# Last quarter of a feed-forward in seven block products: shared sums taken into the residual ahead of the sixth product, and the final gain multiplied onto each half row before the row's scale

## The chip, the cores and the metric

The kernel runs on one core of a Trainium2 chip. The metric is the device time of one execution in microseconds (us); the median of three runs of the kernel before is 855.49 us.

## The reference

One layer of a streaming encoder on 512 rows of 1024 channels, all in float32: three attention branches are gated and merged, projected and added to the residual `h`; then comes a feed-forward sub-layer, and at the end a normalisation of every row. Only the last two matter here:

```python
u2 = rmsnorm(h, g_ffn[l])
h = h + jnp.square(jax.nn.relu(u2 @ w_ff1[l])) @ w_ff2[l]      # D_FF = 4096
...
return rmsnorm(h, g_final)        # h * rsqrt(mean(h*h) + EPS) * g_final
```

## The kernel before

**Precision.** A float32 product is made of three matmuls: each operand is split into a rounded part "hi" and a rest "lo" (`split`: ScalarE casts, VectorE subtracts, lines 202 and 203), and `mm3` (lines 150 to 152) adds hi·hi, hi·lo and lo·hi in one accumulator. Before TensorE can work on a weight tile of 128x1024 numbers, the tile must be loaded, cast by ScalarE (`hi`) and subtracted by VectorE (`lo`). There are three buffers for `hi` and three for `lo`.

**The feed-forward.** The 4096 inner channels are taken in four quarters, `q` = 0 to 3. Within a quarter both multiplications are done on 2x2 blocks with seven block products in place of eight (Strassen's scheme in Winograd's form), so that block sums of operands and results take the place of one product. For the second multiplication the result is the residual itself: `C(i, j, t)` is the half row (512 channels) number `j` of row tile `2*i + t` of `h`; the four tiles of 128 rows are `hN[0]` to `hN[3]`, written h0 to h3 below. `second_product` goes through the products in the order `SECOND` = 1, 2, 5, 3, 6, 7, 4. Each is 24 matmuls of 128x512 numbers: two weight tiles (`i` = 0, 1) of 12 matmuls each, which serve the row tiles `t` = 0 and then `t` = 1. The very last product (n = 4 of the last quarter) is run the other way about: all 12 matmuls of `t` = 0, then all 12 of `t` = 1, so both weight tiles are wanted within its first 7 matmuls.

**Where results go.** `evac` takes a finished product out of its accumulator. Products 1 and 5 stay in PSUM over all four quarters (`held`); products 6 and 7 are summed in the tiles `R6[t]` and `R7[t]` until the third quarter, and R7 is added to the residual ahead of the last quarter. In the last quarter, with M1 to M7 for the products (M1 and M5 over all quarters), R6 becomes M1 - R6 at product 1; at product 6 the tiles E = R6 - M6 and G = M5 - E are made, and G is added to `C(0, 1)` and `C(1, 1)`, E to `C(1, 0)`; at product 7, M7 is taken from `C(1, 1)` and added to `C(1, 0)`.

**The end of a row.** `finish(t, c, n)` is called once for each half row when its last sum is in (n = 0 for the first half that is done, n = 1 for the second). It squares the half on ScalarE, with the sum of the squares going to `hss` (`sumsq`, line 824). The first half is multiplied by `g_final` (`gl`) on VectorE. At the second half the mean goes to `ms` (VectorE, line 831) and its power -1/2 to `rr` (GpSimd, line 832); then VectorE multiplies the second half by `rr` and `gl` in one instruction (line 1057), ScalarE multiplies the first half by `rr` (line 1059), and each sends its half to `out`, by the queue of SyncE and by ScalarE's own.

**What sets the order.** TensorE's order is that of the code. On the other engines a scheduler orders the instructions when the program is built; on the chip each engine runs its queue in that order and waits, at an instruction whose input is not there, with all that is behind it. Two other things hang on VectorE's splits in this stretch: the weights of products 5, 6, 7 and 4 are sums of blocks, which GpSimd's queue makes by DMAs that add into the tiles `b11` and `b12` (line 1114) as soon as VectorE's subtraction has read the sum before.

Of the kernel before, what the change touches and what calls it, by code (L numbers as in the profile page):

```python
# [14 lines left out]
ALU = mybir.AluOpType  # L15
AX = mybir.AxisListType

P = 128
D = 1024
# [42 lines left out]
def hybrid_block(ctx, tc, chunks, wst, xT, memT, xN, cols, gffn, gfin, wup, cst, out):  # L62
    nc = tc.nc
# [758 lines left out]
    def sumsq(sq, src, t, c, n):  # L822

        nc.scalar.activation(sq, src[:, 512 * c:512 * c + 512], AF.Square, accum_out=hss[:, t, n:n + 1])
        if n == 0:
            nc.vector.tensor_scalar(hss[:, t, 0:1], hss[:, t, 0:1], 1.0 / D, EPS, op0=ALU.mult, op1=ALU.add)

    def rms_tile(pool_, t):
        ms = pool_.tile([P, 1], F32, tag="ms", name=nm("ms"), bufs=2)
        r = pool_.tile([P, 1], F32, tag="rr", name=nm("rr"), bufs=2)  # L830
        nc.vector.tensor_scalar(ms, hss[:, t, 1:2], 1.0 / D, hss[:, t, 0:1], op0=ALU.mult, op1=ALU.add)
        nc.gpsimd.tensor_tensor(r, ms, mhalf[:, :1], op=ALU.pow)
        return r

# [2 lines left out]
    with pool("outp") as op_:  # L837
# [50 lines left out]
        def half(j, i, ks=range(KT)):  # L888
            sl = slice(256 * i, 256 * i + 256)
            for k in ks:  # L890
                mm3(first[j][:, sl], ws[j][0][:, k, :], ws[j][1][:, k, :], *(x[:, 2 * (k // 4) + i, k % 4, :] for x in u2),
                    k == 0, k == KT - 1)
# [9 lines left out]
        half(1, 0, range(4, KT))  # L902
        half(0, 1)
        half(1, 1)

# [7 lines left out]
    with pool("ff") as yp:  # L915
# [9 lines left out]
        def scratch():  # L925
            return yp.tile([P, S], F32, tag="sq", name=nm("sq"), bufs=2)
# [118 lines left out]
                first_evac(n, i, ps)  # L1045


        def finish(t, c, n):

            sumsq(scratch(), hN[t], t, c, n)  # L1050
            h = [hN[t][:, 512 * g:512 * g + 512] for g in range(2)]
            g_ = [gl[:, 512 * g:512 * g + 512] for g in range(2)]
            if n == 0:
                nc.vector.tensor_tensor(h[c], h[c], g_[c], op=ALU.mult)
            else:
                r = rms_tile(yp, t)
                nc.vector.scalar_tensor_tensor(h[c], h[c], r, g_[c], op0=ALU.mult, op1=ALU.mult)
                nc.sync.dma_start(out[t * P:(t + 1) * P, 512 * c:512 * c + 512], h[c])
                nc.scalar.mul(h[1 - c], h[1 - c], r)
                nc.scalar.dma_start(out[t * P:(t + 1) * P, 512 - 512 * c:1024 - 512 * c], h[1 - c])  # L1060

        def C(i, j, t):
            return hN[2 * i + t][:, 512 * j:512 * j + 512]
# [1 line left out]
        def evac(q, n, t, ps):  # L1065
            last = q == NQ - 1
            if n == 1 and last:
                x = scratch()
                nc.scalar.copy(x, ps)
                add(C(0, 0, t), x)  # L1070
                sub(R6[t], x, R6[t])
            if n == 2:
                add(C(0, 0, t), ps)
                if last:
                    finish(t, 0, 0)
            if n == 3:
                add(C(0, 1, t), ps)
            if n in (6, 7) and not last:
                R = (R6 if n == 6 else R7)[t]
                if q == 0:  # L1080
                    nc.scalar.copy(R, ps)
                else:
                    add(R, ps)
            if n == 6 and last:
                E, G = R6[t], s1[t]
                sub(E, E, ps)
                sub(G, held[5][t], E)
                add(C(0, 1, t), G)
                finish(t, 1, 1)
                add(C(1, 1, t), G)  # L1090
                add(C(1, 0, t), E)
            if n == 7 and last:
                add(C(1, 1, t), ps, ALU.subtract)
                finish(2 + t, 1, 0)
                add(C(1, 0, t), ps)
            if n == 4:
                add(C(1, 0, t), ps)
                if last:
                    finish(2 + t, 0, 1)

# [154 lines left out]
```

## Time and profile before

| | |
|---|---|
| three runs | 855.39, 855.49, 856.64 us |
| profiled execution | 854.4 us, of which the span from the first to the last instruction is 852.6 us |
| busy in the span | TensorE 831.8 us (98%), VectorE 554.9 us (65%), ScalarE 438.9 us (51%), GpSimd 97.3 us (11%) |
| the chain that ended last | TensorE 86%, VectorE 6%, ScalarE 3%, DMA 3% of the span |

The profiled execution lies 1.1 us under the median of the runs; differences are taken against its own time and then carried to the median. A start in the timeline is counted from the first instruction; products 2, 5, 3, 6, 7, 4 of the last quarter run from about 808.5 us to 843 us. On VectorE an instruction of 128x512 numbers lasts 0.68 us in the profile but the next one starts 0.60 us after it, since two neighbours overlap a little; where instructions are queued, the distance of the starts is what one costs.

### The profile page before, as it was taken

The numbers are of one execution on the slowest core, as the hardware profiler recorded it, in microseconds if no ns is written. First come the engines' busy times: TensorE is split into PE (matmuls) and PEld (weight loads), VectorE is DVE, ScalarE is ACT, GpSimd is POOL, SyncE is SP. The second block draws the span as 40 slices with busy tenths as digits, with TensorE's granted clock in tenths as the row PEclk, the third lists the DMA queues.
The fourth block names the chain that finished last, engine by engine and source line by source line (L and its number), as shares of the span: only waits on it lengthen the run. The fifth ranks groups of instructions, "written<-read, shape, count | busy, mean of one in ns | idle before, by whom it ended". The sixth has DMA issues, their size and how long they took to land.

```text
span 852.6 us, 11738 instructions
## 1 busy us (share of the span) xinstructions
PE 831.8 (98%) x4473; PEld 708.0 (83%) x4473; DVE 554.9 (65%) x886; ACT 438.9 (51%) x703; POOL 97.3 (11%) x114
## 2 busy tenths in 40 slices
PE   7899999999999999999999999999999999999994
PEld 5768788888888888787888889888998899889983
DVE  5784667856344546475444446857689668877897
ACT  8764656755333333132333335655577467646754
POOL 5100000000000022222121100001001100110011
PEclk9999999999999999999999999999999999999998
DMA  8435665553646547156322421948756875895553
GB/s 319 154 124 191 181 211 160 153 194 118 178 127 182 185 125 223 50 173 181 141 102 95 148 100 39 280 111 200 238 192 157 214 244 166 188 246 196 149 90 108
DMA packets 35993, 141.40 MB, mean 166 GB/s; under 512 B 4448, under 2 KB 5408, under 8 KB 34208
## 3 DMA queue, kind: packets, MB, share of 16 engines
q1 hardware_dynamic: 27424, 93.44, 30.7%
q0 software_dynamic: 6720, 41.95, 23.0%
q10 hardware_dynamic: 1792, 5.26, 1.7%
q8 instruction: 35, 0.57, 0.3%
q14 instruction: 22, 0.18, 0.1%
HBM read 138.50 MB, written 27.30 MB: 194 GB/s over the span
## 4 chain that ended last, share of the span: by engine, by line
PE 86%; DVE 6%; ACT 3%; DMA 3%; issue 2%; SPq 0%; POOL 0%; POOLq 0%; ACTq 0%; DVEq 0%
PE mm L150 23%; PE mm L151 23%; PE mm L152 23%; PE a L151 3%; PE a L150 3%; PE a L152 3%; DMA nFb<-dF 1%; DVE h L932 1%; PE a L767 1%; DVE lo L203 1%; DMA raw<-in_wst_dram 1%; PE a L784 1%; DMA memr<-in_memT_dram 1%; PE a L527 1%; PE a L526 1%
## 5 line engine op out<-in xcount | busy, mean ns | idle before, releaser
L142 DVE TENSOR_TENSOR wlo<-raw,whi 128x1024 fp32r<-128x1024 f32 x79 | 100.5, 1276 | 99.0 <-ACT whi L141 98.3
L141 ACT CAST whi<-raw 128x1024 fp32r<-128x1024 f32 x79 | 83.0, 1053 | 127.9 <-PE mm L151 102.6
L150 PE MATMUL mm<-uhi,whi 128*128 128x512 f32 x352 | 139.8, 397 | 0.0
L152 PE MATMUL mm<-uhi,wlo 128*128 128x512 f32 x352 | 137.7, 391 | 0.2 <-DVE wlo L142 0.2
L151 PE MATMUL mm<-ulo,whi 128*128 128x512 f32 x352 | 137.6, 391 | 0.0
L202 ACT CAST hi<-raw 128x1024 fp32r<-128x1024 f32 x58 | 60.8, 1049 | 44.5 <-PE mm L151 31.7
L203 DVE TENSOR_TENSOR lo<-raw,hi 128x1024 fp32r<-128x1024 f32 x58 | 70.9, 1222 | 17.6 <-ACT hi L202 17.6
L152 PEld LDWEIGHTS mm<-uhi,wlo 128*128 128x128 f32 x352 | 66.2, 188 | 14.8 <-DVE wlo L142 0.6
L150 PEld LDWEIGHTS mm<-uhi,whi 128*128 128x128 f32 x352 | 66.3, 188 | 13.6 <-issue 0.7
L151 PEld LDWEIGHTS mm<-ulo,whi 128*128 128x128 f32 x352 | 66.3, 188 | 12.9
L203 DVE TENSOR_TENSOR lo<-b,hi 128x1024 fp32r<-128x1024 f32 x40 | 48.8, 1222 | 26.0 <-ACT hi L202 26.0
L202 ACT CAST hi<-b 128x1024 fp32r<-128x1024 f32 x40 | 41.9, 1048 | 44.5 <-PE mm L152 30.4
L151 PE MATMUL mm<-lo,ch 128*128 128x512 f32 x160 | 62.5, 391 | 0.9 <-DVE lo L203 0.9
L152 PE MATMUL mm<-hi,cl 128*128 128x512 f32 x160 | 62.3, 389 | 0.0
L150 PE MATMUL mm<-hi,ch 128*128 128x512 f32 x160 | 62.3, 389 | 0.0
L1114 POOL DMA_DIRECT2D b<-in_wst_dram x32 | 27.6, 864 | 273.8 <-DVE lo L203 230.0
L152 PE MATMUL mm<-u2h,lo 128*128 128x256 f32 x192 | 54.3, 283 | 0.0
L151 PE MATMUL mm<-u2l,hi 128*128 128x256 f32 x192 | 54.3, 283 | 0.0
L150 PE MATMUL mm<-u2h,hi 128*128 128x256 f32 x192 | 54.3, 283 | 0.0
L150 PE MATMUL mm<-u2sh,hi 128*128 128x256 f32 x144 | 40.8, 283 | 0.0
L151 PE MATMUL mm<-u2sl,hi 128*128 128x256 f32 x144 | 40.8, 283 | 0.0
L152 PE MATMUL mm<-u2sh,lo 128*128 128x256 f32 x144 | 40.8, 283 | 0.0
(349 smaller groups left out, 1936.5 us busy)
## 6 DMA issues: line engine op xcount, KB each, us to landing
raw<-in_wst_dram SPq DMA_DIRECT2D x122, 512.0 KB
b<-in_wst_dram POOLq DMA_DIRECT2D x32, 512.0 KB, 5.3
T<-in_wst_dram POOLq DMA_DIRECT2D x12, 1024.0 KB, 8.4
raw<-T SPq DMA_DIRECT2D x24, 512.0 KB
b<-in_wst_dram SPq DMA_DIRECT2D x16, 512.0 KB
nFb<-dF ACTq DMA_DIRECT2D x8, 512.0 KB
xr<-in_xT_dram SPq DMA_DIRECT2D x4, 512.0 KB
h<-in_xN_dram SPq DMA_DIRECT2D x4, 512.0 KB
```

Source lines behind the costliest of these rows:

```text
L141: cast = nc.scalar.copy(hi, raw)
L142: nc.vector.tensor_tensor(lo, raw, f(hi), op=ALU.subtract)
L150: nc.tensor.matmul(ps, lh, rh, start=start, stop=False)
L151: nc.tensor.matmul(ps, lh, rl, start=False, stop=False)
L152: nc.tensor.matmul(ps, ll, rh, start=False, stop=stop)
L202: nc.scalar.copy(hi, src)
L203: return nc.vector.tensor_tensor(lo, src, f(hi), op=ALU.subtract).ins
L526: nc.tensor.matmul(po[:, q0:], vv, PTh[:, c0:c0 + w], start=n == 0, stop=False)
L527: nc.tensor.matmul(po[:, q0:], vv, PTl[:, c0:c0 + w], start=False, stop=n == 3)
L767: nc.tensor.matmul(ps[:, t, :], kk[:, sl], qq[:, sl], start=True, stop=True)
L784: nc.tensor.matmul(po[r, t, :], qpos[e][:, 64 * c:64 * c + 64], prev[:, c, :], start=False, stop=True)
L1114: nc.gpsimd.dma_start(to[i], wst[index["B", q, i, x]], accum_op=ALU.add)
```

## The change

Four things are changed, all in the last quarter, and no matmul is among them.

1. M1 is copied into `R7[t]`, which is free by then; R6 is left as it is and M1 - R6 goes to `R7[t]`, and is added to `C(1, 0)` at once. When product 5 is done, M5 - R7 is made and added to `C(0, 1)` and `C(1, 1)`. Both stand ahead of product 6.
2. At product 6 only M6 itself is left: ScalarE copies it to `R6[t]` and it is added to `C(0, 1)`. At product 7, M7 - M6 is made, taken from `C(1, 1)` and added to `C(1, 0)`.
3. `finish` multiplies each half by `gl` into another tile (`od` for h0 and h1, `ev` for h2 and h3) while ScalarE squares the half; at the second half VectorE multiplies that tile by `rr` alone, and ScalarE does the same to the first half's tile. `scalar_tensor_tensor` goes out.
4. The addition of the last product to `C(1, 0)` of h3 is placed behind the mean (`ms`) of h2.

```diff
--- before.py
+++ after.py
@@ -825,10 +825,12 @@
         if n == 0:
             nc.vector.tensor_scalar(hss[:, t, 0:1], hss[:, t, 0:1], 1.0 / D, EPS, op0=ALU.mult, op1=ALU.add)
 
+    ms_end = [None]
+
     def rms_tile(pool_, t):
         ms = pool_.tile([P, 1], F32, tag="ms", name=nm("ms"), bufs=2)
         r = pool_.tile([P, 1], F32, tag="rr", name=nm("rr"), bufs=2)
-        nc.vector.tensor_scalar(ms, hss[:, t, 1:2], 1.0 / D, hss[:, t, 0:1], op0=ALU.mult, op1=ALU.add)
+        ms_end[0] = nc.vector.tensor_scalar(ms, hss[:, t, 1:2], 1.0 / D, hss[:, t, 0:1], op0=ALU.mult, op1=ALU.add).ins
         nc.gpsimd.tensor_tensor(r, ms, mhalf[:, :1], op=ALU.pow)
         return r
 
@@ -1045,19 +1048,21 @@
                 first_evac(n, i, ps)
 
 
+        hgs = {}
+
         def finish(t, c, n):
 
             sumsq(scratch(), hN[t], t, c, n)
-            h = [hN[t][:, 512 * g:512 * g + 512] for g in range(2)]
-            g_ = [gl[:, 512 * g:512 * g + 512] for g in range(2)]
-            if n == 0:
-                nc.vector.tensor_tensor(h[c], h[c], g_[c], op=ALU.mult)
-            else:
+            sl = slice(512 * c, 512 * c + 512)
+            hg = hgs[t, c] = (ev if t > 1 else od)[t % 2][:, n, :]
+            nc.vector.tensor_tensor(hg, hN[t][:, sl], gl[:, sl], op=ALU.mult)
+            if n:
                 r = rms_tile(yp, t)
-                nc.vector.scalar_tensor_tensor(h[c], h[c], r, g_[c], op0=ALU.mult, op1=ALU.mult)
-                nc.sync.dma_start(out[t * P:(t + 1) * P, 512 * c:512 * c + 512], h[c])
-                nc.scalar.mul(h[1 - c], h[1 - c], r)
-                nc.scalar.dma_start(out[t * P:(t + 1) * P, 512 - 512 * c:1024 - 512 * c], h[1 - c])
+                nc.vector.tensor_scalar(hg, hg, r, None, op0=ALU.mult)
+                nc.sync.dma_start(out[t * P:(t + 1) * P, sl], hg)
+                other = hgs[t, 1 - c]
+                nc.scalar.mul(other, other, r)
+                nc.scalar.dma_start(out[t * P:(t + 1) * P, 512 - 512 * c:1024 - 512 * c], other)
 
         def C(i, j, t):
             return hN[2 * i + t][:, 512 * j:512 * j + 512]
@@ -1065,10 +1070,16 @@
         def evac(q, n, t, ps):
             last = q == NQ - 1
             if n == 1 and last:
-                x = scratch()
+                x = R7[t]
                 nc.scalar.copy(x, ps)
                 add(C(0, 0, t), x)
-                sub(R6[t], x, R6[t])
+                sub(x, x, R6[t])
+                add(C(1, 0, t), x)
+            if n == 5 and last:
+                x = R7[t]
+                sub(x, ps, x)
+                add(C(0, 1, t), x)
+                add(C(1, 1, t), x)
             if n == 2:
                 add(C(0, 0, t), ps)
                 if last:
@@ -1082,19 +1093,21 @@
                 else:
                     add(R, ps)
             if n == 6 and last:
-                E, G = R6[t], s1[t]
-                sub(E, E, ps)
-                sub(G, held[5][t], E)
-                add(C(0, 1, t), G)
+                nc.scalar.copy(R6[t], ps)
+                add(C(0, 1, t), ps)
                 finish(t, 1, 1)
-                add(C(1, 1, t), G)
-                add(C(1, 0, t), E)
             if n == 7 and last:
-                add(C(1, 1, t), ps, ALU.subtract)
+                x = R6[t]
+                sub(x, ps, x)
+                add(C(1, 1, t), x, ALU.subtract)
+                add(C(1, 0, t), x)
                 finish(2 + t, 1, 0)
-                add(C(1, 0, t), ps)
             if n == 4:
-                add(C(1, 0, t), ps)
+                if last and t:
+                    with tc.issue_after(ms_end[0]):
+                        add(C(1, 0, t), ps)
+                else:
+                    add(C(1, 0, t), ps)
                 if last:
                     finish(2 + t, 0, 1)
```

The order of TensorE's matmuls is the same in both programs, and the queues of VectorE, ScalarE, GpSimd and SyncE are the same up to product 1 of the last quarter. The rows below are instructions in the order of an engine's queue: line, operation, output and inputs. A name's digits ahead of the last underscore are the program's (h0 is `hN[0]`, R70 `R7[0]`, b110 `b11[0]`, `od1` the second tile of `od`, `lo` and `hi` the parts of a weight tile); the number behind it is a buffer's.

VectorE around product 5 (weight tiles from `b110` and `b111`), up to the first weight tile of product 3 (from `raw`). Before:

```order
L932 TENSOR_TENSOR h1_3639<-h1_3639,sq_1057_7187 128x512
L929 TENSOR_TENSOR R61_4583<-sq_1057_7187,R61_4583 128x512
L929 TENSOR_TENSOR s11_4577<-ev1_4573,s11_4577 128x512
L203 TENSOR_TENSOR lo_1069_7253<-b110_4086,hi_1068_7252 128x1024
L203 TENSOR_TENSOR cl0_4580<-ev0_4572,ch0_4578 128x512
L932 TENSOR_TENSOR h0_3638<-h0_3638,mm_1058_7197 128x512
L929 TENSOR_TENSOR od1_4575<-od1_4575,s11_4577 128x512
L203 TENSOR_TENSOR lo_1071_7270<-b111_4087,hi_1070_7269 128x1024
L203 TENSOR_TENSOR cl1_4581<-s11_4577,ch1_4579 128x512
L932 TENSOR_TENSOR h1_3639<-h1_3639,mm_1059_7198 128x512
L203 TENSOR_TENSOR cl1_4581<-ev1_4573,ch1_4579 128x512
L203 TENSOR_TENSOR lo_1076_7294<-raw_1074_7291,hi_1075_7293 128x1024
```

and with the change:

```order
L932 TENSOR_TENSOR R70_4584<-R70_4584,R60_4582 128x512
L932 TENSOR_TENSOR R71_4585<-R71_4585,R61_4583 128x512
L932 TENSOR_TENSOR od1_4575<-od1_4575,s11_4577 128x512
L203 TENSOR_TENSOR cl0_4580<-ev0_4572,ch0_4578 128x512
L935 TENSOR_TENSOR h0_3638<-h0_3638,mm_1056_7197 128x512
L203 TENSOR_TENSOR lo_1069_7270<-b111_4087,hi_1068_7269 128x1024
L203 TENSOR_TENSOR cl1_4581<-s11_4577,ch1_4579 128x512
L935 TENSOR_TENSOR h2_3640<-h2_3640,R70_4584 128x512
L935 TENSOR_TENSOR h3_3641<-h3_3641,R71_4585 128x512
L935 TENSOR_TENSOR h1_3639<-h1_3639,mm_1057_7198 128x512
L203 TENSOR_TENSOR cl1_4581<-ev1_4573,ch1_4579 128x512
L203 TENSOR_TENSOR lo_1074_7300<-raw_1072_7297,hi_1073_7299 128x1024
```

The subtractions that make M1 - R6 have moved from ahead of `b110`'s tile to behind it, and the additions of M1 - R6 to h2 and h3 are new ahead of product 3's first tile.

VectorE at the two weight tiles of the last product (`b110` and `b111` as inputs). Before:

```order
L203 TENSOR_TENSOR lo_1103_7447<-b110_4086,hi_1102_7446 128x1024
L932 TENSOR_TENSOR h0_3638<-h0_3638,s10_4576 128x512
L932 TENSOR_TENSOR h2_3640<-h2_3640,s10_4576 128x512
L932 TENSOR_TENSOR h1_3639<-h1_3639,s11_4577 128x512
L932 TENSOR_TENSOR h3_3641<-h3_3641,s11_4577 128x512
L203 TENSOR_TENSOR lo_1105_7452<-b111_4087,hi_1104_7451 128x1024
L932 TENSOR_TENSOR h2_3640<-h2_3640,mm_1092_7395 128x512
```

and with the change:

```order
L935 TENSOR_TENSOR h0_3638<-h0_3638,mm_1078_7335 128x512
L935 TENSOR_TENSOR h1_3639<-h1_3639,mm_1079_7336 128x512
L203 TENSOR_TENSOR lo_1101_7451<-b110_4086,hi_1100_7450 128x1024
L1058 TENSOR_TENSOR od0_4574<-h0_3638,gl_6901 128x512
L1058 TENSOR_TENSOR od1_4575<-h1_3639,gl_6901 128x512
L833 TENSOR_SCALAR ms_1085_7370<-hss_593_3642 128x1
L203 TENSOR_TENSOR lo_1103_7456<-b111_4087,hi_1102_7455 128x1024
L932 TENSOR_TENSOR R60_4582<-mm_1090_7397,R60_4582 128x512
```

Where four additions of G stood between the two weight tiles there are two products with `gl` and the mean of h0; the additions stand earlier.

ScalarE's last instructions, from the last square of h2 (`sq ... <-h2`) on; `rr` is the row's scale. Before:

```order
L824 ACTIVATE sq_1106_7468,hss_593_3642<-h2_3640 128x512
L824 ACTIVATE sq_1109_7491,hss_593_3642<-h3_3641 128x512
L1059 ACTIVATE h2_3640<-h2_3640,rr_1108_7471 128x512
L1060 DMA out_0_dram<-h2_3640 128x512
L1059 ACTIVATE h3_3641<-h3_3641,rr_1111_7494 128x512
L1060 DMA out_0_dram<-h3_3641 128x512
```

and with the change:

```order
L824 ACTIVATE sq_1104_7472,hss_593_3642<-h2_3640 128x512
L1064 ACTIVATE ev0_4572<-ev0_4572,rr_1106_7476 128x512
L824 ACTIVATE sq_1107_7496,hss_593_3642<-h3_3641 128x512
L1065 DMA out_0_dram<-ev0_4572 128x512
L1064 ACTIVATE ev1_4573<-ev1_4573,rr_1109_7500 128x512
L1065 DMA out_0_dram<-ev1_4573 128x512
```

The square of h3's last half has moved behind ScalarE's multiplication of h2's first half by `rr`.

## The prediction

> **What bounds the kernel now.** I read the page first, then the chain that ended last, and then, since the change lies in the last 45 us, the timeline of each engine there. On the page, the busy times and the shares of the chain:
>
> ```profile
> PE 831.8 (98%) x4473; PEld 708.0 (83%) x4473; DVE 554.9 (65%) x886; ACT 438.9 (51%) x703; POOL 97.3 (11%) x114
> ...
> PE 86%; DVE 6%; ACT 3%; DMA 3%; issue 2%; SPq 0%; POOL 0%; POOLq 0%; ACTq 0%; DVEq 0%
> ```
>
> Over the whole span TensorE is the bound. The stretch that the change edits is another matter: these are the busy times from the first VectorE row that differs to the start of the last addition, and what VectorE waited for in it.
>
> ```profile
> 809.35:844.43 35.08, 32.60 (x141) 25.87 (x140) 34.26 (x54) 19.54 (x32) 4.56 (x6) 1.00 0.40 83
> ...
> DVE lo L203 <- ACT hi L202: 0.8, 1, 0.8
> ```
>
> VectorE is busy 34.26 of 35.08 us, and its only wait is 0.82 us for one cast. Here VectorE is full, and TensorE follows it. VectorE's rows of the timeline at the places used below:
>
> ```profile
> 809.35 0.68 DVE L932 TENSOR_TENSOR h<-h,sq 128x512 f32<-128x512 f32 x1
> 809.95 0.68 DVE L929 TENSOR_TENSOR R<-sq,R 128x512 f32<-128x512 f32 x1
> ...
> 817.63 0.68 DVE L203 TENSOR_TENSOR cl<-ev,ch 128x512 fp32r<-128x512 f32 x1
> 818.23 1.21 DVE L203 TENSOR_TENSOR lo<-raw,hi 128x1024 fp32r<-128x1024 f32 x1
> 819.37 0.14 DVE L826 TENSOR_SCALAR hss<-hss 128x1 f32<-128x1 f32 x1
> 819.43 0.68 DVE L1054 TENSOR_TENSOR h<-h,gl 128x512 f32<-128x512 f32 x1
> ...
> 835.01 2.49 DVE L932 TENSOR_TENSOR h<-h,s 128x512 f32<-128x512 f32 x4
> 837.42 1.22 DVE L203 TENSOR_TENSOR lo<-b,hi 128x1024 fp32r<-128x1024 f32 x1
> ...
> 839.15 0.21 DVE L831 TENSOR_SCALAR ms<-hss 128x1 f32<-128x1 f32 x1
> 839.27 1.27 DVE L932 TENSOR_TENSOR h<-h,mm 128x512 f32<-128x512 f32 x2
> ...
> 843.17 0.74 DVE L1057 SCALAR_TENSOR_TENSOR h<-h,rr,gl 128x512 f32<-128x512 f32 x1
> 843.83 0.68 DVE L1054 TENSOR_TENSOR h<-h,gl 128x512 f32<-128x512 f32 x1
> 844.43 0.68 DVE L932 TENSOR_TENSOR h<-h,mm 128x512 f32<-128x512 f32 x1
> 845.03 0.20 DVE L831 TENSOR_SCALAR ms<-hss 128x1 f32<-128x1 f32 x1
> 845.90 0.21 DVE L831 TENSOR_SCALAR ms<-hss 128x1 f32<-128x1 f32 x1 [0.67 <-ACT sq L824]
> ...
> 847.21 0.75 DVE L1057 SCALAR_TENSOR_TENSOR h<-h,rr,gl 128x512 f32<-128x512 f32 x1 [0.44 <-POOL rr L832]
> ```
>
> The distance of two starts is what a queued instruction costs: 0.60 us for 512 numbers with two inputs, 1.14 for a weight tile's `lo`, 0.66 for the fused multiply (L1057), 0.06 for `hss`, 0.12 for `ms`. TensorE in the same stretch:
>
> ```profile
> 819.60 0.40 PE L151 MATMUL mm<-lo,ch 128*128 128x512 f32 x1
> ...
> 822.50 0.50 PE L151 MATMUL mm<-lo,ch 128*128 128x512 f32 x1
> ...
> 836.01 0.39 PE L150 MATMUL mm<-hi,ch 128*128 128x512 f32 x1
> ...
> 838.69 0.50 PE L151 MATMUL mm<-lo,ch 128*128 128x512 f32 x1 [0.93 <-DVE lo L203]
> ...
> 842.49 0.39 PE L152 MATMUL mm<-hi,cl 128*128 128x512 f32 x1
> ```
>
> From 822.50 to 836.01 there are 59 matmuls, 0.229 us each. The last product's eighth matmul should start at 836.01 + 7 x 0.229 = 837.6 and starts at 838.69: TensorE loses 1.1 us, since the second weight tile's `lo` (837.42) is queued behind four additions of G (835.01). Its last matmul is done by 842.9, yet the last addition starts only at 844.43: VectorE is 1.5 us behind. ScalarE and GpSimd at the end:
>
> ```profile
> 840.10 0.72 ACT L1059 ACTIVATE h<-h,rr 128x512 f32<-128x512 f32 x1
> 840.73 0.62 ACT L824 ACTIVATE sq<-h 128x512 f32<-128x512 f32 x1
> ...
> 845.14 0.63 ACT L824 ACTIVATE sq<-h 128x512 f32<-128x512 f32 x1 [1.20 <-DVE h L932]
> 845.68 0.19 ACT L824 ACTIVATION_READ_ACCUMULATOR sq<-h 128x1 f32 x1
> 845.90 0.72 ACT L1059 ACTIVATE h<-h,rr 128x512 f32<-128x512 f32 x1
> ...
> 845.32 0.55 POOL L832 TENSOR_TENSOR rr<-ms,cst_s 128x1 f32<-128x1 f32 x1 [4.01 <-DVE ms L831]
> 846.19 0.98 POOL L832 TENSOR_TENSOR rr<-ms,cst_s 128x1 f32<-128x1 f32 x1 [0.33 <-DVE ms L831]
> ```
>
> So the end hangs on one chain: VectorE's queue down to the last addition, then square, `ms`, `rr`, the last multiply, which ends at 847.96, and 4.67 us of output DMA and closing to the end of the span (852.63).
>
> **The change, part by part.** TensorE's order is unchanged. I count VectorE's rows from the first that differs to the last addition.
>
> *Shared sums.* A row tile pair needed, at products 1, 6 and 7, nine instructions per `t` (two, five and two); now products 1, 5, 6 and 7 take ten (three, three, one and three). That is one more for each `t`: 2 x 0.60 = +1.20 us. The two copies of M6 go to ScalarE, like the copies of M1 before:
>
> ```profile
> 807.74 0.58 ACT L1069 COPY sq<-a 128x512 f32<-128x512 f32 x1
> ```
>
> Two of 0.58 us fit there (busy 19.54 of 35.08 us); behind them stands the cast for the last product's first tile, whose `lo` VectorE reaches over 1 us later. They cost nothing while that holds, at most 1.2 us otherwise.
>
> *Gain.* Before the last addition VectorE had four products with `gl` (0.60) and two fused ones (0.66). Now it has seven products with `gl` and two multiplies by `rr` alone: +1.80 us and 2 x (x - 0.66). For x the trace has multiplies by a column elsewhere in the kernel, four in a row of 256 numbers and one of 512:
>
> ```profile
> 234.71 1.14 DVE L658 TENSOR_SCALAR Pm<-Pm,ri 128x256 f32<-128x256 f32 x4
> ...
> 198.06 0.48 DVE L553 TENSOR_SCALAR sg<-sg,cols_s 128x512 f32<-128x512 f32 x1
> 198.46 0.28 DVE L502 RECIPROCAL ri<-rs 128x1 f32<-128x1 f32 x3
> ```
>
> Behind the one of 512 the next starts 0.40 us later. That is the same shape, so x = 0.40, -0.52 us for the two. It is not under 0.28, a quarter of the four (1.14 / 4), which have half the numbers, and not over the 0.66 of the fused form.
>
> *Order.* The `ms` of h2 now stands ahead of the last addition: +0.12 us.
>
> Work added: 1.20 + 1.80 - 0.52 + 0.12 = +2.60 us, in a queue that has 0.82 us of idle time. That idle time came at product 7's second weight tile, whose cast waited for TensorE to free a buffer; in the new queue eight more 512-wide instructions stand ahead of this tile, 4.8 us, while TensorE is some 1.7 us late (below), so I take the idle time as used up. The last addition starts 2.60 - 0.82 = 1.78 us later, at 846.21.
>
> *TensorE on the way.* Ahead of product 3's first `lo` stand 13 instructions of 512 and two `lo` instead of 11 and two: it starts 1.20 us later, at 819.43, and is ready at 820.64, while TensorE wants it at 819.60. So TensorE now waits 1.0 us there. By the same count the next three `lo` are ready at 823.64, 826.64 and 829.58 (each time 1.14 and three instructions of 0.60 further on), and TensorE, at 12 matmuls of 0.229 = 2.75 us a tile, wants them about 0.2 us earlier: 1.7 us in all. The wait at 838.69 goes: ahead of that `lo` there are now 28.5 us of queue from 809.35, so it is ready by 839.1, and TensorE, which starts the product about 1.7 us later than 836.01, wants it at about 839.3. TensorE ends near 843.4, far ahead of 846.21: VectorE hides all of it.
>
> *GpSimd's queue.* The DMA that adds up the last weight tile now starts behind a `lo` that ends at 829.6 in place of 826.0. Such DMAs land within:
>
> ```profile
> DMA to landing us min/median/max: 5.0/5.4/6.8
> ```
>
> so by 836.7 with the slowest; the cast and then VectorE's turn at 837.85 follow. No cost.
>
> *The end of the chain.* On ScalarE the last square (h3) now stands behind the multiply of h2's half by `rr`. From the last addition's start at 846.21: `ms` of h2 0.12 earlier, 846.09; its `rr` 0.84 later as before (845.03 to 845.87), 846.93; ScalarE's multiply from 846.96, the square 0.63 behind it (840.10 to 840.73), 847.59; its sum 0.73 later (845.14 to 845.87), 848.32; `ms` 848.35; `rr` 1.27 later as before for the last one (845.90 to 847.17), 849.62; the multiply on ScalarE, 0.72 and the step of 0.03, to 850.37. VectorE's own last multiply, 0.48 in place of 0.75, ends earlier and saves nothing. So 850.37 - 847.96 = +2.41 us: 1.78 from VectorE's queue and 0.63 from the multiply ahead of the square.
>
> One difference could speak for the change: the instructions of VectorE that read PSUM fall from 14 to 12. The rows that weigh this are the groups of the two kinds:
>
> ```profile
> L932 DVE TENSOR_TENSOR h<-h,mm 128x512 f32<-128x512 f32 x28 | 18.4, 679 | 0.0
> L932 DVE TENSOR_TENSOR h<-h,R 128x512 f32<-128x512 f32 x6 | 3.9, 683 | 0.0
> ```
>
> 679 ns with an input in PSUM and 683 without: no difference, and I count none. [...]
>
> **Sum.** 854.4 + 2.4 = 856.8 us for a profiled execution. The median of the three runs lies 1.09 above the profiled one, so I predict 855.49 + 2.4 = 857.9 us, 0.28% more. A measurement of this kernel can tell about 0.2%, 1.7 us, from no change.
>
> **The rivals.**
>
> *Cheaper end, within 0.2%.* The queue term holds, but `rr` of h3 takes the 0.84 us of its fellows instead of 1.27, and the multiply by `rr` costs VectorE 0.28: +2.41 - 0.43 - 0.24 = +1.7, and if ScalarE's multiply does not hold up the square, +1.1: 856.6 to 857.2 us. For it: three of four `rr` are short. Against it: the long one was the last one, and the queue order is fixed. Chance 0.18.
>
> *Faster.* Additions moved forward run where VectorE would have waited, VectorE has caught up when the last product is done, and the end follows TensorE, which no longer waits. The last addition would start at 842.9 less the 1.1 us of the lost wait, 841.8, 2.6 us earlier; with 0.6 for the square's place, -2.0: 853.5 us. It decides if VectorE has some 5 us of free time (2.6 added, 2.6 to catch up) in the stretch; the row of busy times shows 0.82. [...] Chance 0.06.
>
> *Slower still.* The idle 0.82 us stays, because a late TensorE frees its buffers late and VectorE waits again for a cast, and `rr` of h2 takes the long 1.27: +2.41 + 0.82 + 0.43 = +3.7: 859.2 us. For it: the same buffers are in use. Against it: VectorE comes to these tiles later than TensorE frees them. Chance 0.08.
>
> That the change does not do what it says can be excluded: the queues show each edit.
>
> **How the numbers follow.** My forecast has 0.68; of this about 0.05 may land below +1.7 through the scatter of the runs (855.39 to 856.64). Slower by over 0.2%: 0.63 + 0.08 + 0.01 of the cheaper end = 0.72; within 0.2%: 0.17 + 0.05 = 0.22; faster: 0.06. The range takes in the cheaper end from +0.9 and reaches to the slower rival: 856.4 to 859.3 us.
>
> **What would show it.** VectorE without a wait from 809 us to the last addition, and that addition near 846.2; TensorE waiting about 1 us at product 3's first `lo` near 820.6, and not at the last product's second tile; the last square behind ScalarE's multiply; the last multiply ending near 850.4. I am wrong if the last addition starts before 845 us, or if VectorE shows waits of over 1 us ahead of it.

## The result

The changed kernel takes 857.94 us (median of 12 runs, 853.60 to 860.40), the kernel before 854.01 us (12 runs, 851.68 to 856.64). The ratio is 1.0043, with a 95% interval of 1.0024 to 1.0062: slower, by 3.7 us as the ratio has it; the two medians lie 3.9 us apart. The forecast was 857.9 us.

The profiled execution of the changed kernel took 854.44 us, with a span of 852.7 us, as long as that of before (852.6). The change is nevertheless in it. I measure it as a *stretch*: from the start of the first VectorE row that differs (the first addition of M1 to h0) to the end of the last multiply by `rr`. Behind the stretch 4.6 to 4.8 us follow in every profile of this study.

The first lines are from the page of the changed kernel: busy time by engine, and the shares of the chain that ended last.

```profile
PE 832.3 (98%) x4473; PEld 708.4 (83%) x4473; DVE 557.1 (65%) x892; ACT 439.9 (52%) x705; POOL 97.8 (11%) x114
...
PE 88%; DVE 6%; ACT 3%; issue 2%; DMA 1%; SPq 0%; POOLq 0%; POOL 0%; ACTq 0%; DVEq 0%
```

Six more instructions on VectorE and two more on ScalarE, as the diff says, and nearly the same chain by engine. Next, the busy times of the changed kernel from the first row of the stretch to the start of the last addition (TensorE, weight loads, VectorE, ScalarE, GpSimd, then clock and DMA):

```profile
807.47:844.25 36.78, 33.34 (x141) 25.74 (x140) 36.78 (x60) 20.73 (x34) 5.40 (x6) 1.00 0.41 86
```

VectorE is busy 36.78 of 36.78 us, where it was 34.26 of 35.08. The 0.82 us of idle time are used up and the last addition stands 1.70 us later. VectorE's rows in the timeline of the changed kernel:

```profile
807.47 1.29 DVE L935 TENSOR_TENSOR h<-h,R 128x512 f32<-128x512 f32 x2
...
838.40 0.49 DVE L1061 TENSOR_SCALAR od<-od,rr 128x512 f32<-128x512 f32 x1
838.80 1.30 DVE L935 TENSOR_TENSOR h<-h,R 128x512 f32<-128x512 f32 x2
...
844.13 0.22 DVE L833 TENSOR_SCALAR ms<-hss 128x1 f32<-128x1 f32 x1
844.25 0.69 DVE L935 TENSOR_TENSOR h<-h,mm 128x512 f32<-128x512 f32 x1
845.01 0.49 DVE L1061 TENSOR_SCALAR ev<-ev,rr 128x512 f32<-128x512 f32 x1
845.41 0.69 DVE L1058 TENSOR_TENSOR ev<-h,gl 128x512 f32<-128x512 f32 x1
846.38 0.21 DVE L833 TENSOR_SCALAR ms<-hss 128x1 f32<-128x1 f32 x1 [0.28 <-ACT sq L824]
```

TensorE's waits in the stretch, from its timeline, and its last matmul:

```profile
818.83 0.50 PE L151 MATMUL mm<-lo,ch 128*128 128x512 f32 x1 [0.95 <-DVE lo L203]
...
830.80 0.47 PE L150 MATMUL mm<-hi,ch 128*128 128x512 f32 x1 [0.20 <-DVE h L935]
...
841.57 0.39 PE L152 MATMUL mm<-hi,cl 128*128 128x512 f32 x1
```

The wait at product 3's first `lo` is there (0.95 us), the one at the last product's second tile is gone, and the last matmul starts 2.68 us ahead of the last addition. ScalarE and GpSimd at the end:

```profile
845.01 0.72 ACT L1064 ACTIVATE ev<-ev,rr 128x512 f32<-128x512 f32 x1 [1.29 <-POOL rr L834]
845.64 0.61 ACT L824 ACTIVATE sq<-h 128x512 f32<-128x512 f32 x1
...
847.25 0.72 ACT L1064 ACTIVATE ev<-ev,rr 128x512 f32<-128x512 f32 x1 [0.91 <-POOL rr L834]
...
836.20 1.40 POOL L834 TENSOR_TENSOR rr<-ms,cst_s 128x1 f32<-128x1 f32 x1 [7.32 <-DVE ms L833]
...
846.67 0.55 POOL L834 TENSOR_TENSOR rr<-ms,cst_s 128x1 f32<-128x1 f32 x1 [1.69 <-DVE ms L833]
```

The last square (845.64) stands behind the multiply by `rr` (845.01). The last `rr` lasts 0.55 us, in the kernel before 0.98; the long one is now the first. The stretch is 847.97 - 807.47 = 40.50 us, against 847.96 - 809.35 = 38.61: +1.89 us.

The two spans are equal because the stretch begins 1.88 us sooner here, and that is no work of the change (e1 below begins where before does). The windows of the two profiles show a part of the reason (the third number from the end is the granted clock), first before, then after:

```profile
0.00:50.00 50.00, 42.93 (x221) 32.16 (x222) 35.66 (x50) 37.65 (x72) 15.39 (x20) 1.00 0.60 212
...
100.00:150.00 50.00, 49.59 (x243) 41.83 (x244) 33.74 (x88) 31.79 (x64) 2.15 (x3) 0.97 0.56 171
```

```profile
0.00:50.00 50.00, 43.10 (x216) 32.51 (x217) 34.32 (x49) 37.59 (x72) 15.49 (x20) 0.97 0.60 211
...
100.00:150.00 50.00, 49.69 (x253) 42.09 (x253) 34.21 (x87) 32.47 (x63) 2.66 (x4) 1.00 0.57 171
```

Either execution loses clock in one 50 us window of its first 150 us, and not in the same one; 0.03 of 50 us is 1.5 us, and early on, where TensorE is not always busy (42.93 of 50 us against 49.59), the loss should cost less. So the clock can, as an estimate from these windows, make up most of the 1.88 us and not all. What makes up the rest is not shown: the mean clock over the whole span is 0.995 in before and in e2 below, and 0.996 in e3, and yet their stretches begin at 809.35, 808.06 and 806.78. One profile's span therefore decides nothing here, while the stretch can be compared.

### The profile page after: what moved, and what is told of

Read it like the earlier page. It is cut to its first block, busy times and chain, and to the rows that moved or that the text cites. A ratio compares the mean times of both kernels' runs of the same rounds, so it can differ in the third digit from the quotient of the medians.

```text
span 852.7 us, 11746 instructions
## 1 busy us (share of the span) xinstructions
PE 832.3 (98%) x4473; PEld 708.4 (83%) x4473; DVE 557.1 (65%) x892; ACT 439.9 (52%) x705; POOL 97.8 (11%) x114
## 4 chain that ended last, share of the span: by engine, by line
PE 88%; DVE 6%; ACT 3%; issue 2%; DMA 1%; SPq 0%; POOLq 0%; POOL 0%; ACTq 0%; DVEq 0%
PE mm L150 24%; PE mm L152 24%; PE mm L151 24%; PE a L151 3%; PE a L150 3%; PE a L152 3%; DVE lo L203 1%; DVE h L935 1%; PE a L767 1%; DMA memr<-in_memT_dram 1%; PE a L784 1%; PE a L527 1%; PE a L526 1%; PE a L778 1%; DVE ut L365 1%
```

## The experiments

The two theories: *the stretch* (the change costs what VectorE's queue and the end of the chain show, 1.9 us, and nothing elsewhere), and *something outside it* (another 2 us, which the measured 3.7 us suggest). All timed comparisons are with the kernel before on the same chip. "Lowest" is the shortest run less the shortest run of before there; before has more runs in most of these comparisons (up to 35), so its shortest may lie a little lower for that alone. The stretch of before was profiled once; the kernels that were profiled again repeat theirs within 0.02 us (after with e1 and e9, e7 with e10).

| | stretch, us | against before | lowest | ratio and interval |
|---|---|---|---|---|
| before | 38.61 | | | |
| after | 40.50 | +1.89 | +1.92 | 1.0043 [1.0024, 1.0062] |
| e1, after again | 40.49 | +1.88 | +2.78 | 1.0051 [1.0032, 1.0070] |
| e9, after a third time | 40.51 | +1.90 | +1.65 | 1.0027 [1.0010, 1.0044] |
| e2, sums alone | 40.83 | +2.22 | +1.77 | 1.0018 [1.0006, 1.0031] |
| e3, gain alone | 39.85 | +1.24 | +1.16 | 1.0023 [1.0008, 1.0037] |
| e4, before without the first gain | 37.12 | -1.49 | -1.33 | 0.9983 [0.9964, 1.0002] |
| e5, after, earlier `lo` | 40.50 | +1.89 | +1.97 | 1.0010 [0.9992, 1.0027] |
| e6, after, square first | 40.13 | +1.52 | +1.86 | 1.0016 [0.9999, 1.0033] |
| e7, before, later additions | 37.97 | -0.64 | -0.42 | 0.9982 [0.9965, 0.9999] |
| e10, the same again | 37.98 | -0.63 | -0.77 | 0.9992 [0.9977, 1.0007] |
| e8, e7 and two products on GpSimd | 39.35 | +0.74 | +0.73 | 0.9999 [0.9980, 1.0018] |
| e11, e7 and two late multiplies | 38.08 | -0.53 | -0.55 | 1.0003 [0.9982, 1.0024] |
| e12, e11 with four `rr` buffers | 37.58 | -1.03 | -0.91 | 1.0000 [0.9980, 1.0021] |

**e1 and e9, the changed kernel again**, without an edit.

> The changed kernel once more, beside the kernel before on the same chip. Measure of the stretch: from the start of the first addition of M1 to h0 on VectorE to the end of the last multiply by rr; before 38.61 us, changed 40.50 us in the profiles so far. My theory (VectorE's queue fills the stretch, what is added to it comes out at its end): the stretch is again 40.3 to 40.9 us, and the time 1.9 to 2.4 us over before (ratio 1.0022 to 1.0028); what was measured beyond that (ratio 1.0043) is the scatter of the runs. Rival (the new waits of TensorE bring something more, such as a lower granted clock): the time is again 3.5 us or more over before (1.004 and up), with mean granted clocks below those of before in most runs.

> The changed kernel a third time. The stretch from the first shared addition on VectorE to the end of the last multiply was 40.50 and 40.49 us in its two profiles and 38.61 us in the one of before. My theory: the change costs these 1.9 us and nothing else; what the two timed comparisons showed above that (1.0043 and 1.0051, 3.7 and 4.3 us) is scatter of the half-clock windows that lie ahead of the stretch, up to 1.7 us apiece, and falls differently in each comparison. Then the stretch is 40.5 again and the ratio is near 1.002 (1.001 to 1.0045). Rival: the changed code costs another 2 us outside the stretch in every run; then the ratio is at 1.004 or above a third time with a stretch of 40.5.

The stretch came out within 0.02 us both times. The profile of e1 happens to lose its clock in the same window as that of before (its windows and its timeline):

```profile
0.00:50.00 50.00, 42.88 (x222) 32.20 (x223) 36.34 (x50) 37.54 (x72) 15.71 (x20) 1.00 0.61 212
...
100.00:150.00 50.00, 49.45 (x243) 41.88 (x244) 33.55 (x87) 31.63 (x63) 2.15 (x3) 0.97 0.57 172
...
809.36 1.28 DVE L935 TENSOR_TENSOR h<-h,R 128x512 f32<-128x512 f32 x2
...
846.16 0.67 DVE L935 TENSOR_TENSOR h<-h,mm 128x512 f32<-128x512 f32 x1
...
849.13 0.72 ACT L1064 ACTIVATE ev<-ev,rr 128x512 f32<-128x512 f32 x1 [0.91 <-POOL rr L834]
```

Here the stretch begins at 809.36, within 0.01 us of before; the last addition stands at 846.16, where the prediction had 846.21, and the span is 854.5 us, 1.9 more than that of before. With equal clock, then, all of the difference lies in the stretch. In e9 two windows lose clock, and its stretch begins at 811.44:

```profile
0.00:50.00 50.00, 44.34 (x213) 33.13 (x214) 33.63 (x48) 36.98 (x71) 15.48 (x20) 0.93 0.59 204
...
100.00:150.00 50.00, 47.68 (x236) 40.18 (x235) 32.99 (x91) 32.19 (x68) 2.15 (x3) 0.97 0.62 188
```

The ratio of e9, 1.0027, is what 2.3 us make, and its interval holds the 1.9 us (1.0022). The rival's 1.004 did not come a third time, though the interval reaches up to it (1.0044).

**e2, the shared sums alone**: `evac` of the changed kernel, with `finish` of the one before.

```diff
-            hg = hgs[t, c] = (ev if t > 1 else od)[t % 2][:, n, :]
-            nc.vector.tensor_tensor(hg, hN[t][:, sl], gl[:, sl], op=ALU.mult)
...
+                nc.vector.scalar_tensor_tensor(h[c], h[c], r, g_[c], op0=ALU.mult, op1=ALU.mult)
```

> Only the order of the shared sums (edits 1, 2 and 4); the end of a row as before. By VectorE's queue: 37 instructions of 512 with two inputs instead of 35, one more mean ahead of the last addition, no idle time, so the last addition 0.4 us later than before from the stretch's start (35.5 us); ScalarE's multiply stands ahead of the last square, +0.2 to 0.7: stretch 39.2 to 39.7 us, +0.6 to +1.1 us in the time. Rival (TensorE's waits at product 3 are what costs): nearly all of the loss is here, stretch 40.2 us or more, since the additions ahead of product 3's first weight tile are the same.

The stretch is 40.83 us, over 1.1 above what was expected. Its VectorE timeline and, behind it, ScalarE's:

```profile
836.92 1.22 DVE L203 TENSOR_TENSOR lo<-b,hi 128x1024 fp32r<-128x1024 f32 x1 [1.48 <-ACT hi L202]
...
832.86 1.05 ACT L202 CAST hi<-b 128x1024 fp32r<-128x1024 f32 x1 [0.66 <-DMA b<-in_wst_dram]
...
835.84 1.05 ACT L202 CAST hi<-b 128x1024 fp32r<-128x1024 f32 x1 [1.31 <-PE mm L152]
```

Without the two extra products VectorE comes early to the last product's second tile and waits 1.48 us for its cast. Both casts waited for the DMAs that add up their tiles. The second row names TensorE, but in the changed kernel the same cast starts 7.69 us ahead of the last matmul (833.88 against 841.57), so TensorE had freed the buffer by 842.17 - 7.69 = 834.48 here, and the tile's DMA, issued at 828.61, took 7.1 us and landed at 835.7. The times from issue to landing of these DMAs, of e2 and then of the changed kernel:

```profile
DMA to landing us min/median/max: 5.2/5.5/7.1
```

```profile
DMA to landing us min/median/max: 5.1/5.3/5.8
```

Less that wait the stretch would be 39.35, in the expected range. The 40.83 lies in the rival's range (40.2 or more), but as far as this one profile shows not for the rival's reason: a late tile held VectorE up, and not TensorE's waits at product 3. That tile's DMA was issued 20.55 us after the start of the stretch, as in the changed kernel, but only 2.3 us behind the one before it, and not 2.9. The second of these two comes 1.1 us behind the first in before, 1.7 in e3 and 2.3 in e2, and there the slowest of the six DMAs takes 6.8, 6.3 and 7.1 us (in before and e2 it is this one); in the changed kernel it comes 2.9 us behind and takes 5.4 us, and in e1, also 2.9 us behind, no one of the six takes more than 5.5. So each half of the change has a wait of its own, and the halves do not add up: 2.2 and 1.2 us alone, 1.9 together.

**e3, the gain alone**: `finish` of the changed kernel, with `evac` of the one before.

```diff
-                nc.vector.scalar_tensor_tensor(h[c], h[c], r, g_[c], op0=ALU.mult, op1=ALU.mult)
...
+            nc.vector.tensor_tensor(hg, hN[t][:, sl], gl[:, sl], op=ALU.mult)
+            if n:
+                r = rms_tile(yp, t)
+                nc.vector.tensor_scalar(hg, hg, r, None, op0=ALU.mult)
```

> Only the multiplication by g_final into another tile and the scale alone (edit 3); the shared sums as before. By VectorE's queue: 37 instructions of 512 with two inputs instead of 35 and two multiplies of 0.40 for two of 0.66, idle time of 0.8 us kept, so the last addition 0.6 us later than before (35.7 us); ScalarE's squares come first here, +0 to 0.4: stretch 39.2 to 39.6 us, +0.6 to +1.0 us in the time. Rival (TensorE's waits): product 3 is not delayed by additions here, only by one product with gl, so no more than +0.2 us.

39.85 us, 0.25 above the range. The queue's busy time to the last addition rose from 34.26 to 34.94, its waits from 0.82 to 1.1 us. At the end GpSimd's two `rr` took 1.49 us (its timeline) while VectorE multiplied by `gl` (VectorE's):

```profile
844.34 1.49 POOL L834 TENSOR_TENSOR rr<-ms,cst_s 128x1 f32<-128x1 f32 x2 [4.09 <-DVE ms L833]
...
844.18 0.68 DVE L1058 TENSOR_TENSOR ev<-h,gl 128x512 f32<-128x512 f32 x1
```

**e4, before without the product of a row's first half and `g_final`**; this leaves the gain out of the first half of every row.

```diff
-            if n == 0:
-                nc.vector.tensor_tensor(h[c], h[c], g_[c], op=ALU.mult)
-            else:
+            if n:
```

> The kernel before without the multiplication of each row's first half by g_final (four instructions of 0.60 us on VectorE left out). My theory (VectorE is behind at the end and sets it): the two that stand before product 7's tile only make the wait for the cast longer (0.8 to 2.0 us), the two behind the last weight tile come off the end: stretch 1.2 us shorter, 37.4 us, and 1.2 us off the time. Rival (the end follows TensorE and its wait at the last product's second tile, which stays): no change, 38.6 us.

Four products less, 2.4 us, gave 1.49 us of stretch (1.2 had been expected): VectorE's idle time to the last addition grew from 0.82 to 33.59 - 31.95 = 1.64 us. VectorE's queue sets the end, and work taken from it comes back in time less what then becomes a wait.

```profile
810.35:843.94 33.59, 32.26 (x141) 25.96 (x140) 31.95 (x51) 19.44 (x32) 4.55 (x6) 1.00 0.40 75
```

**e5, after, with the additions of M1 - R6 behind product 3's first `lo`**, to take away TensorE's wait there (M5 - R7 goes to another free tile for that).

```diff
-                add(C(1, 0, t), x)
+                pend.append(partial(add, C(1, 0, t), x))
...
+                    if q == NQ - 1 and n == 3:
+                        with tc.issue_after(lo_end[0]):
+                            while pend:
+                                pend.pop(0)()
```

> The changed kernel with the additions of M1 - R6 to h2 and h3 placed behind product 3's first lo (M5 - R7 goes to another free tile for that). VectorE has the same work in the stretch, but TensorE's new wait of about 1 us at that tile goes. My theory (VectorE's queue sets the end): stretch again 40.5 us and the time as the changed kernel's, 1.9 us over before or, if the runs repeat, 3.5 to 4.5. Rival (TensorE's new wait costs, by itself or by a lower granted clock): the time falls to within 2.5 us of before, by 1.0 us or more below the changed kernel's.

The wait did not go, it moved to product 3's second tile (TensorE's timeline):

```profile
821.70 0.50 PE L151 MATMUL mm<-lo,ch 128*128 128x512 f32 x1 [1.20 <-DVE lo L203]
```

The stretch is the same to 0.01 us with the wait at one place or at the other. That TensorE's waits are hidden behind VectorE fits, but a kernel with the changed sums and without such a wait was not run.

**e6, after, with ScalarE's multiply by `rr` of h2 behind the last square.**

```diff
+                elif t == 2:
+                    held["scale"] = scale
+                else:
+                    with tc.issue_after(sq_end[0]):
+                        held["scale"]()
+                    scale()
```

> The changed kernel with ScalarE's multiply of h2's half placed behind the last square of h3. My theory: the square starts 0.65 us sooner after the last addition, but the mean of h3 then waits for VectorE's own product with gl in front of it, so 0.37 us come off: stretch 40.1 us. Rival (the place of the square is hidden): 40.5 us. The time itself can't tell 0.4 us.

40.13 us, 0.37 less, as expected: of the 0.63 us of that multiply so much lies on the end of the chain; VectorE's own instructions between the last addition and the last mean cover the rest, since that mean follows them without a wait (VectorE's timeline of e6):

```profile
848.65 0.69 DVE L1060 TENSOR_TENSOR ev<-h,gl 128x512 f32<-128x512 f32 x1
849.25 0.21 DVE L835 TENSOR_SCALAR ms<-hss 128x1 f32<-128x1 f32 x1
```

**e7 and e10, before, with G's additions to `C(1, 1)`, the subtraction of M7 and what follows placed behind the last product's second `lo`.**

```diff
+                def rest():
+                    add(C(1, 1, t), s1[t])
+                    add(C(1, 1, t), ps, ALU.subtract)
+                    finish(2 + t, 1, 0)
+                    add(C(1, 0, t), ps)
+                pend.append(rest)
...
+                    if q == NQ - 1 and n == 4:
+                        with tc.issue_after(lo_end[0]):
+                            while pend:
+                                pend.pop(0)()
```

> The kernel before with G's additions to h2 and h3, and what follows on these halves, placed behind the last product's second lo, so that TensorE no longer waits 1.1 us there; VectorE's work is the same. My theory: VectorE is behind all the same, so TensorE ends 1 us earlier in the stretch without the end following; the order behind it (the last addition of h3 ahead of its first half's product with gl) gives 0.6 us: stretch 38.0 us. Rival (the end follows TensorE): 37.5 us or less.

> The kernel before with G's additions to the second row pair, the subtraction of M7 and what follows placed behind the last product's second lo, a second time. Theory: VectorE's queue is then full to the last addition, and the wait of TensorE at that tile is gone; the stretch is 38.0 us again (before 38.6), ratio 0.999 by the stretch, 0.9982 in the first comparison. Rival: the first comparison's gain was scatter; the stretch is 38.6 and the ratio 1.000.

TensorE has no wait in the last product any more, yet that is not where the 0.64 us come from. The row of busy times up to the last addition, of e7:

```profile
808.21:842.62 34.41, 32.31 (x141) 25.89 (x140) 33.60 (x53) 19.13 (x32) 4.52 (x6) 1.00 0.41 85
```

VectorE still idles 0.81 us, so its queue is not full, though e10's theory had it so. What changed is that one instruction fewer stands ahead of the last addition, h3's product with `gl`: 35.08 - 34.41 = 0.67. Both comparisons lie below 1, one interval only just. This order beats the changed kernel; against the one before its gain is 0.64 us in the profiles and not settled by the times.

**e8, e7 with the products of h2 and h3 with `gl` on GpSimd.**

```diff
+                if t < 2:
+                    nc.vector.tensor_tensor(h[c], h[c], g_[c], op=ALU.mult)
+                else:
+                    with tc.issue_after(rr_end[0]):
+                        nc.gpsimd.tensor_tensor(h[c], h[c], g_[c], op=ALU.mult)
```

> The same, with the products with gl of h2's and h3's first halves given to GpSimd behind the rr of h1. A try for a version that beats both. My theory: 1.2 us less in VectorE's queue behind the last lo, so the last addition is limited by what is in front of it: stretch 36.6 to 37.2 us, 1.4 to 2.0 us under before. Rival (GpSimd's 1.3 to 1.5 us each delay rr of h2 and h3, or slow VectorE down): 38 us or more.

39.35 us: 1.4 longer than e7, though VectorE has two products less. The rows of e8 (GpSimd, VectorE), then the same two multiplies in e7:

```profile
842.18 2.95 POOL L1061 TENSOR_TENSOR h<-h,gl 128x512 f32<-128x512 f32 x2 [0.93 <-ACT sq L824]
...
842.45 3.24 DVE L1064 SCALAR_TENSOR_TENSOR h<-h,rr,gl 128x512 f32<-128x512 f32 x2
```

```profile
840.04 1.42 DVE L1058 SCALAR_TENSOR_TENSOR h<-h,rr,gl 128x512 f32<-128x512 f32 x2
```

While GpSimd multiplies, VectorE's two fused multiplies take 3.24 us and not 1.42.

**e11 and e12, e7 with the fused multiplies of h0 and h1 behind the last mean**; e12 has four buffers for `rr` in place of two.

```diff
+                if t < 2:
+                    pend2.append(scale)
+                else:
+                    if t == 3:
+                        with tc.issue_after(ms_end[0]):
+                            while pend2:
+                                pend2.pop(0)()
+                    scale()
...
-        r = pool_.tile([P, 1], F32, tag="rr", name=nm("rr"), bufs=2)
+        r = pool_.tile([P, 1], F32, tag="rr", name=nm("rr"), bufs=4)
```

> As e10, and in addition the two fused multiplies of h0 and h1 on VectorE, 0.7 us each, are placed behind the last mean of squares. Theory: VectorE is full up to the last addition, so the last addition comes up to 1.4 us sooner, unless the last product's end holds it: TensorE's last matmul started 31.92 us after the stretch's start in e7, and the last addition cannot start before it has ended. The two multiplies then fill VectorE's wait for the last rr (0.7 to 1.1 us) and spill over by 0.3 to 0.7 us. Stretch 37.2 to 37.6 us, ratio 0.998. Rival: TensorE's end holds the last addition already, and the two multiplies only make the end longer; stretch 38.3 or more.

> As e11 with four buffers for rr in place of two. In e11 the last addition came 33.10 us after the stretch's start (34.44 in e10), yet the stretch was 38.08: GpSimd's first late rr started only at 843.77, behind VectorE's delayed multiply (842.89), which reads the rr whose buffer it takes. Theory: with a buffer for each rr the two rr run under VectorE's two multiplies (842.43 + 0.54 for the means, 0.3 to the first rr, 1.1 for the two: 844.3), VectorE goes on without a wait from 842.89 for four multiplies of 0.70 and ends 37.5 us after the start; ratio 0.9985 to 0.999. Rival: something else than the buffers holds the rr back, such as GpSimd being slowed by VectorE's two-input multiplies; the stretch stays at 38.1.

In e11 the last addition came 33.10 us after the start, 1.3 sooner, but all of it was given back (a stretch of 38.08 against 37.97 in e7, where 37.2 to 37.6 was expected), because `rr` of h2 waited for the multiply whose buffer it takes. In e12, with a buffer for each, that wait is gone and VectorE runs through. GpSimd's row of e11, then VectorE's of e12:

```profile
843.77 1.44 POOL L834 TENSOR_TENSOR rr<-ms,cst_s 128x1 f32<-128x1 f32 x2 [5.06 <-DVE h L1061]
```

```profile
846.07 2.73 DVE L1061 SCALAR_TENSOR_TENSOR h<-h,rr,gl 128x512 f32<-128x512 f32 x4
```

37.58 us, with 37.5 expected; the times do not tell this 1.0 us from nothing (1.0000 [0.9980, 1.0021]).

## Why the prediction was right, point by point

- **VectorE's queue: right.** Last addition +1.78 predicted, +1.70 measured; the idle 0.82 us used up, as said; the multiply by a column costs 0.40 (838.40 to 838.80), as taken from the other line.
- **TensorE: right.** About 1.0 us predicted at product 3's first `lo`, 0.95 measured; none at the last product's second tile; its last matmul starts 34.10 us after the stretch's start, 2.7 us ahead of the last addition. The next three tiles cost less than the 0.2 us each that was predicted: their first matmul with `lo` comes 0.37, 0.32 and 0.27 us behind the one before (821.47 to 821.84, 824.51 to 824.83, 827.50 to 827.77), where the usual step is 0.23. One wait of 0.20 us came later.
- **GpSimd's queue: right for this order.** No cast waits for the last tile's DMA in the changed kernel. (The sum in the prediction is off: 829.6 + 6.8 is 836.4 and not 836.7; nothing hangs on it.) In e2 the same term costs 1.48 us.
- **The last square behind ScalarE's multiply: right**, by the rows and by e6.
- **The last `rr`: wrong, by 0.43 us.** The step "`rr` 1.27 later as before for the last one" carried a duration from the old order into the new one. From the last mean's start to its end it is now 846.67 + 0.55 - 846.38 = 0.84 us. In the kernel before, the last `rr` (846.19, 0.98 us) ran against the fused multiply of h2; in the new order VectorE has nothing left to do at that point. That was the "cheaper end", given 0.18, as far as `rr` goes. So the end of the chain grew by 0.19 us and not by 0.63: 1.70 + 0.19 = +1.89 in place of +2.41.
- **PSUM: no difference again.** The groups of the changed kernel by line (busy time and mean ns of one), with an input in PSUM and without:

```profile
L935 DVE TENSOR_TENSOR h<-h,mm 128x512 f32<-128x512 f32 x26 | 17.1, 683 | 0.0
L935 DVE TENSOR_TENSOR h<-h,R 128x512 f32<-128x512 f32 x16 | 10.4, 691 | 0.0
```

  683 ns and 691: no difference, as counted.

- **The absolute places** (the last addition near 846.2, the last multiply near 850.4) hold only where the stretch starts at 809.35. In the first profile the addition stands at 844.25, ahead of the 845 that I had named as my refutation; in e1, with the start of before, at 846.16. They should have been counted from the stretch's start.
- **The size.** The profiles show +1.9 us and the lowest runs +1.92, the first comparison's ratio +3.7. The forecast's +2.4 lies between, and that it meets the median to 0.1 us is chance: it was 0.5 us too high for the stretch (the last `rr`), and the median of before fell from 855.49 to 854.01 with more runs. Over all kernels the lowest runs follow the stretch (table), within 0.5 us except in e1, which has six runs only (0.9). The rest of the 3.7 us stands in how far the runs lie above their lowest. Why this is more for the changed kernel (three ratios above the 1.0022 of the stretch, two of them with intervals that leave it out, from 1.0024 and 1.0032) is not shown: e1, with its clock lost where that of before is, has no cost outside the stretch, and e5 and e6, nearly the same kernels, came out at 1.0010 and 1.0016. The granted clock goes with a part of it. Its mean over the runs was 0.9922 in e1 against 0.9936 for before beside it; in e9 it was 0.9928 against 0.9926, and there the mean times differ by 2.3 us only. In the first comparison it was 0.9909, and the clocks of before beside it are not on record. Whether the change lowers the clock or chance did stays open.

## What to carry to other kernels

A kernel can keep TensorE busy for 98% of its span and be bound by VectorE in its last 35 us, as this one; an edit there is priced by counting what stands in that engine's queue ahead of the last needed result, less the idle time it can fill. Do not carry a duration from one order into another before having seen what ran beside it (the last `rr`: 0.98 us in one order, 0.55 in the other). Where the effect is 2 us in 850 and the runs scatter by 5, measure the stretch from the first changed row to the end in the profile, and let the times only confirm it.

## What the runs showed of the hardware

**GpSimd and VectorE slow each other here.** Of the 36 `rr` in the stretch that the fourteen profiles show singly, 27 take 0.55 or 0.56 us and nine 0.98 to 1.41. Each of the nine starts while VectorE is in an instruction with two inputs from SBUF, a `lo` or a fused multiply, and none of the 27 does. The long ones end 0.40 to 0.42 us behind that instruction: in the kernel before 846.03 + 0.74 = 846.77 for the fused multiply of h2 and 846.19 + 0.98 = 847.17 for `rr` (the multiply that waits for it starts at 847.21); in the changed kernel the first `rr` (836.20 + 1.40 = 837.60) behind a `lo` that ends at 835.95 + 1.23 = 837.18. Next to an addition that reads PSUM (844.25 in the changed kernel) it stays at 0.55 us (844.43). The multiply of before, then the rows of the changed kernel:

```profile
846.03 0.74 DVE L1057 SCALAR_TENSOR_TENSOR h<-h,rr,gl 128x512 f32<-128x512 f32 x1
```

```profile
835.95 1.23 DVE L203 TENSOR_TENSOR lo<-b,hi 128x1024 fp32r<-128x1024 f32 x1
...
844.43 0.55 POOL L834 TENSOR_TENSOR rr<-ms,cst_s 128x1 f32<-128x1 f32 x1 [5.89 <-DVE ms L833]
```

The other way about, e8 differs from e7 only in GpSimd's two products, and VectorE's multiplies go from 1.42 to 3.24 us. The nine long `rr` all began second, while VectorE's instruction was under way; VectorE's multiplies in e8 start at 842.45, behind GpSimd's first product (842.18). That the last `rr` was short in the changed kernel because no such instruction of VectorE ran beside it is read from these rows; no run changed that alone.

**The clock is lost early, and not alike from one execution to the next**: 0.97 in one 50 us window in before, after and e1 (in after not the same one), 0.93 and 0.97 in two of them in e9, where the stretch began 2.1 us later than in before. In these four profiles all other windows up to 846 us show 1.00. Looked at more closely, the granted clock is 0.50 from 13.0 to 16.0 us in after, and 0.62 and 0.52 in the two windows of 2 us from 100 us on in before.
